# Modulation's accumulators transposed whole, its adds on VectorE alone, and the norms' tiles in strict order

## The chip, the cores and the metric

The kernel runs on one core of a Trainium2 chip. TensorE (PE) multiplies, VectorE (DVE), ScalarE (ACT) and GpSimd (POOL) work on tiles in SBUF, the first two also on PSUM, and SyncE (SP) issues most DMAs. Each engine takes its instructions strictly in the order in which the program lists them; a wait of one instruction holds up all behind it on that engine. The metric is the device time of one execution in microseconds (us).

## The reference

Two layers work on 512 latent tokens (`x`) and 256 context tokens (`ctx`), 1024 channels, all float32. Each layer is a half-step SwiGLU FFN, a token mixer (convolution, pooling, attention) and a second half-step FFN; before each comes a modulated RMS norm. The change touches how the modulation is computed and when the norms' tiles are made:

```python
m  = (jax.nn.silu(c)     @ w_mod[l] + b_mod[l]).reshape(B, N_MOD, D_MODEL)   # 1024 x 9216 weights a layer
mc = (jax.nn.silu(c_ctx) @ w_mod[l] + b_mod[l]).reshape(1, N_MOD, D_MODEL)
...
h = rms_norm(x, g) * (1 + m[:, 3*i + 1, None]) + m[:, 3*i, None]
x = x + 0.5 * m[:, 3*i + 2, None] * ((silu(a) * b) @ w2)        # a, b = split(h @ w1)
```

`m` and `mc` are matrix-vector products: two vectors (`c` and `c_ctx`) against the same 18 blocks of 512 columns in each layer.

## The kernel before

All activations lie transposed, as 8 tiles of 128 channels by 768 tokens. A product is made of three passes of a rounded type, so each operand is split into a high part (ScalarE casts) and a low part (VectorE subtracts): weights `stg` into `hl`, normed activations into `hhi` and `hlo`, the FFN's hidden values, which go through DRAM (`u`, `tmp` -> `gd` -> `gr`), into `gs`.

One FFN runs in stages. `ffn_in_first` and `ffn_in` make the first tiles of 128 hidden columns plainly, 96 matmuls of 512 or 256 columns a tile; `ffn_quad` makes the later ones with 7 products of half the tokens in place of 8, 84 matmuls of 384 columns a tile, from sums of token halves (`t0` to `t3`) that `sums_open` builds on VectorE (tag "T", tiles `tu` and `t`). `plain(l, s)` says where the quads begin: after tile 4 in the very first FFN, after tile 3 in the next two; the last FFN, which has no context tokens, is plain throughout. Then `ffn_out_main` multiplies 18 of the 22 hidden tiles by w2: two passes over 4 output tiles each, 18 x 2 x 4 = 144 groups of 6 matmuls (three of 512 columns, three of 256). In this text a main is one such stage of one of the first three FFNs. `ffn_out_last` adds the last 4 hidden tiles, updates `x` tile by tile and starts the next norms.

The modulation runs beside the first three FFNs, except 4 blocks that `start` makes at the beginning. `mod_chain` walks 12, 10 and 10 blocks in them. A block is 16 steps, 8 slices of 128 rows of w_mod times 2 vectors: each step multiplies a slice `wm` (128 x 512) by a column of silu(c) and adds it to an accumulator `acc` (128 x 2 x 512). The two steps of the first slice are written by ScalarE; the others are one SCALAR_TENSOR_TENSOR on VectorE, or, in the mains alone and where GpSimd has nothing to do, a product on ScalarE into `mt` and an add on GpSimd. `mod_fold` then sums `acc` over its 128 partitions: two DMAs on SP's queue bring one half of the partitions beside the other, two adds of 64 partitions on VectorE halve it (`fold`), 4 transposes on TensorE turn it into one PSUM bank (`mbank` in a main), and one TENSOR_REDUCE of 512 columns makes the 8 sums (`small`), which `mod_put` writes to `M`. All blocks of an FFN have to be done before its `ffn_out_last`: `flush_tag("mod")` stands at the end of `ffn_out_main`.

The order of instructions is made when the program is built. `Clock` estimates when each engine is free, and `Builder` keeps a heap of events (`at`, `after`, `defer`) that it takes as the estimated time goes by (`take`); an event for "DVE" is put off while VectorE is booked. Tags say what an event belongs to: "mod", "T", ("norm", stream). The streams of the norms are XA and XB (256 latent tokens each) and C (context), of falling priority in `PRIO`. On the chip no such choice is left: what the builder put in a row stays in it. All engines' calls pass through one helper, so every instruction has line 68, and rows are told apart by their tiles.

Of the kernel before, what the change touches and what calls it, by code (L numbers as in the profile page):

```python
# [16 lines left out]
P = 128  # L17
# [189 lines left out]
class Builder:  # L207
# [3 lines left out]
    def __init__(self, tc, nc, ins, out):  # L211
# [16 lines left out]
        self.spreads = 0  # L228

# [53 lines left out]
    def take(self, e):  # L283
        t, _, tag, fn, eng = e
        if eng is not None:
# [3 lines left out]
            if tag == "mod" and any(e[2] == "T" or e[2] in self.PRIO for e in self.events):  # L289

                self.at(max(t, self.now()) + 0.5, fn, tag, eng)
                return
# [48 lines left out]
    def plain(self, l, s):  # L341
        return NF - 1 if l == s == 1 else PLAIN + 1 + (l + s == 0)
# [227 lines left out]
    def mod_add(self, acc, k, v, src, pool=False):  # L570
# [4 lines left out]
        elif pool:  # L575
            t = self.tile(self.gopool, [P, 512], "mt", 2)
            nc.scalar.activation(t, src, AF.Copy, scale=sc)
            nc.gpsimd.tensor_tensor(acc[:, v], acc[:, v], t, OP.add)
        else:
            nc.vector.scalar_tensor_tensor(out=acc[:, v], in0=src, scalar=sc, in1=acc[:, v], op0=OP.mult, op1=OP.add)  # L580

    def mod_fold(self, l, cb, acc, then):

        nc = self.nc
        f = self.tile(self.wm_pool, [P, 512], "fold", 1)
        lower, upper = HALVES
        nc.sync.dma_start(f[lower], acc[upper, 0])
        nc.sync.dma_start(f[upper], acc[lower, 1])
        self.folds += 1

        def add():
            nc.vector.tensor_tensor(f[lower], f[lower], acc[lower, 0], OP.add)
            nc.vector.tensor_tensor(f[upper], f[upper], acc[upper, 1], OP.add)
            self.after([f], turn, "mod", 4.0)

        def turn():
            ps = self.mbank if self.mbank is not None else self.bank()
            self.hold(ps)
            self.transposes(ps, [f[:, b * P:(b + 1) * P] for b in range(4)])
            self.after([ps], lambda: put(ps), "mod")  # L600

        def put(ps):
            r = self.small(8).rearrange("p (v b) -> p v b", v=2)
            nc.vector.tensor_reduce(r, ps.rearrange("p (b v c) -> p v b c", b=4, v=2), axis=AX.X, op=OP.add)
            self.hold(ps, -1)
            self.mod_put(l, cb * 4, 4, r)
            self.folds -= 1
        self.after([f], add, "mod", 2.0)
# [10 lines left out]
    def mod_chain(self, blocks):  # L619
# [10 lines left out]
        def add(i, pool=False):  # L630
# [3 lines left out]
            self.mod_add(acc[0], k, v, w[i // 4][:, k % 2, :], pool)  # L634
# [5 lines left out]
            else:  # L640
                self.after([acc[0]], lambda: self.mod_fold(l, cb, acc[0], lambda: then(i + 1)), "mod", 1.0)

        def then(i):
            if i == len(steps):
                return
            if i // 4 not in w or (i % 16 == 15 and self.folds):

                self.defer(0.5, lambda: then(i), "mod")
                return
# [1247 lines left out]
```

## Time and profile before

| what | value |
|---|---|
| time, 3 runs | median 2686.82 us (2681.61 to 2687.28) |
| the profiled execution | time 2688.29 us, span 2686.5 us, mean granted TensorE clock 0.976 |
| busy share of the span | PE 95%, DVE 74%, ACT 42%, POOL 16% |
| chain that ended last | PE 70%, DVE 15%, DMA 10%, the rest 5% |
| mains (windows used below) | 375 to 578, 1281 to 1464, 1850 to 2018 us |

The profiled execution is 1.5 us above the median. A granted clock of 1 is 2.4 GHz; what TensorE gets otherwise is 1.2 GHz, so a mean of 0.92 over a stretch says that it had the lower level for 16% of it. The page counts a PE that is busy with pipelined matmuls as busy, whatever their pace.

### The profile page before, as it was taken

How to read it: one execution, taken by the hardware profiler on the slowest of the kernel's cores; microseconds unless marked ns; L12 is line 12 of the kernel's file. 1: busy time of each engine (PE TensorE's matmuls, PEld its weight loads, DVE VectorE, ACT ScalarE, POOL GpSimd, SP SyncE). 2: the span in 40 equal slices, each digit the busy share in tenths (PEclk: the TensorE clock that was granted, in tenths of full speed). 3: DMA queues.
4: the chain of work that ended last, by engine and by line, in shares of the span. 5: the costliest groups of instructions: out<-in, count | busy, mean ns of one | idle time of the engine just before them, and what ended most of it. 6: DMA issues, size and time to landing. Idle time of an engine off the chain costs nothing.

```text
span 2686.5 us, 40400 instructions
## 1 busy us (share of the span) xinstructions
PE 2543.1 (95%) x15100; PEld 2315.4 (86%) x15100; DVE 1982.2 (74%) x3553; ACT 1135.0 (42%) x2251; POOL 416.8 (16%) x460
## 2 busy tenths in 40 slices
PE   7999998879998999999989899999999999999998
PEld 4999987769987999999778899998788987888886
DVE  7888878767778698888777888887887787633355
ACT  4433335435445444333443443334454554422332
POOL 1000014341110200000332100002242111000001
PEclk9999999989999999999999899999999999999999
DMA  8334476734322343435765234347762422333362
GB/s 321 108 120 137 129 265 212 219 108 138 100 75 77 105 151 107 133 120 191 260 204 167 99 112 128 121 146 259 226 218 69 134 92 73 130 123 120 122 200 91
DMA packets 138133, 397.03 MB, mean 148 GB/s; under 512 B 15888, under 2 KB 34448, under 8 KB 136912
## 3 DMA queue, kind: packets, MB, share of 16 engines
q1 hardware_dynamic: 127728, 362.72, 42.0%
q0 software_dynamic: 10208, 31.73, 3.1%
q8 instruction: 118, 1.93, 0.3%
q14 instruction: 79, 0.65, 0.1%
HBM read 334.35 MB, written 53.22 MB: 144 GB/s over the span
## 4 chain that ended last, share of the span: by engine, by line
PE 70%; DVE 15%; DMA 10%; issue 2%; ACT 2%; SPq 1%; DVEq 0%; POOL 0%; ACTq 0%
PE b L68 70%; DMA gr<-gd 7%; DVE hl L68 3%; DVE acc L68 2%; DVE gs L68 2%; DMA wm<-in_wm_dram 1%; DVE hlo L68 1%; DVE small L68 1%; DVE x L68 1%; DVE tmph L68 1%; ACT gs L68 1%; DVE tu L68 1%; DVE fold L68 1%; SPq L68 1%; DMA x<-xd 1%
## 5 line engine op out<-in xcount | busy, mean ns | idle before, releaser
L68 PE MATMUL b<-hhi,hl 128*128 128x256 f32 (+2 forms) x4408 | 1145.7, 340 | 15.4 <-ACT hhi L68 7.0
L68 PEld LDWEIGHTS b<-hhi,hl 128*128 128x128 f32 x4408 | 776.4, 191 | 82.2 <-ACT hhi L68 8.2
L68 PE MATMUL b<-hlo,hl 128*128 128x512 f32 (+2 forms) x2204 | 731.0, 337 | 1.3 <-DVE hlo L68 1.2
L68 PE MATMUL b<-gs,hl 128*128 128x512 f32 (+1 forms) x3888 | 707.5, 343 | 10.9 <-DVE gs L68 4.4
L68 PEld LDWEIGHTS b<-gs,hl 128*128 128x128 f32 x3888 | 608.0, 193 | 101.8 <-DVE gs L68 6.6
L68 DVE TENSOR_TENSOR hl<-stg,hl 128x512 fp32r<-128x512 f32 x762 | 553.2, 746 | 117.1 <-ACT hl L68 116.2
L68 ACT CAST hl<-stg 128x512 fp32r<-128x512 f32 x762 | 450.5, 618 | 390.4 <-PE b L68 306.8
L68 PE MATMUL b<-t,hl 128*128 128x384 f32 x2544 | 468.0, 340 | 0.0
L68 PEld LDWEIGHTS b<-t,hl 128*128 128x128 f32 x2544 | 449.7, 188 | 0.2 <-DVE u L68 0.2
L68 PEld LDWEIGHTS b<-hlo,hl 128*128 128x128 f32 x2204 | 420.8, 191 | 31.8 <-DVE hlo L68 2.6
L68 DVE SCALAR_TENSOR_TENSOR acc<-wm,sc,acc 128x512 f32<-128x512 f32 x312 | 267.7, 873 | 30.0 <-DMA wm<-in_wm_dram 20.4
L68 ACT CAST gs<-gr 128x768 fp32r<-128x768 f32 (+1 forms) x160 | 124.7, 780 | 346.1 <-DMA gr<-gd 312.1
L68 DVE TENSOR_TENSOR gs<-gr,gs 128x768 fp32r<-128x768 f32 (+1 forms) x160 | 166.7, 1047 | 139.3 <-ACT gs L68 138.8
L68 POOL TENSOR_TENSOR acc<-acc,mt 128x512 f32<-128x512 f32 x136 | 206.7, 1522 | 293.9 <-ACT mt L68 251.8
L68 POOL DMA_DIRECT2D gd<-u x106 | 57.3, 541 | 729.4 <-DVE u L68 728.9
L68 DVE TENSOR_TENSOR u<-u,b 128x384 f32<-128x384 f32 x159 | 87.8, 552 | 86.0 <-PE b L68 85.0
L68 POOL TENSOR_TENSOR sqs<-sqs,tmph 128x256 f32<-128x256 f32 x102 | 79.2, 791 | 348.9 <-ACT tmph L68 347.4
L68 DVE SCALAR_TENSOR_TENSOR x<-b,M,x 128x256 f32<-128x256 f32 (+1 forms) x160 | 87.3, 571 | 56.6 <-PE b L68 56.1
L68 ACT ACTIVATE mt<-wm,sc 128x512 f32<-128x512 f32 x136 | 95.7, 718 | 52.9 <-DMA wm<-in_wm_dram 46.6
L68 POOL TENSOR_TENSOR bt<-E,con 128x256 f32<-128x256 f32 x64 | 47.2, 738 | 393.8 <-DVE small L68 339.5
L68 POOL DMA_DIRECT2D gd<-tmp x35 | 19.1, 547 | 445.1 <-DVE tmp L68 431.5
L68 DVE TENSOR_REDUCE small<-b 128x1 f32<-128x256 f32 (+5 forms) x130 | 63.4, 487 | 33.2 <-PE b L68 32.4
(117 smaller groups left out, 2050.5 us busy)
## 6 DMA issues: line engine op xcount, KB each, us to landing
stg<-in_w_dram SPq DMA_DIRECT2D x328, 512.0 KB
wm<-in_wm_dram SPq DMA_DIRECT2D x128, 512.0 KB
gr<-gd SPq DMA_DIRECT2D x120, 384.0 KB
gd<-u POOLq DMA_DIRECT2D x106, 192.0 KB, 2.2
xd<-x SPq DMA_DIRECT2D x32, 384.0 KB
x<-xd SPq DMA_DIRECT2D x32, 384.0 KB
gr<-gd SPq DMA_DIRECT2D x40, 256.0 KB
gd<-tmp POOLq DMA_DIRECT2D x35, 256.0 KB, 3.6
```

Source lines behind the costliest of these rows:

```text
L68: return f(*a, **k)
```

## The change

In three places it does this. The modulation's adds after the first slice are all on VectorE: the product on ScalarE into `mt` and the add on GpSimd are gone, and with them the rule in `mod_chain` that chose them. `mod_fold` makes no fold: `acc` is transposed as it is, 4 transposes and one TENSOR_REDUCE for the first vector, then 4 and one for the second, in a main both in the one bank `mbank`. The norms: while a stream's tiles are being made, events for VectorE of a lower priority (other streams' tiles, the token sums, modulation) are put off, at most three low parts (`rest`) are left pending, and the builds of the token sums are events for VectorE like the tiles. In the first FFN one tile more is plain, 5 where there were 4.

```diff
@@ -286,9 +288,10 @@
             if self.nc.end[eng] > max(t, self.now()) + (1.2 if tag in self.PRIO else 0.2):
                 self.at(self.nc.end[eng], fn, tag, eng)
                 return
-            if tag == "mod" and any(e[2] == "T" or e[2] in self.PRIO for e in self.events):
-
-                self.at(max(t, self.now()) + 0.5, fn, tag, eng)
+            if tag == "mod" and any(e[2] == "T" or e[2] in self.PRIO for e in self.events) \
+                    or any(self.PRIO.get(tag, 9) > self.PRIO[o] for o in self.tiling):
+
+                self.at(max(t, self.now()) + 0.4, fn, tag, eng)
                 return
         if eng is not None and tag in self.PRIO:
 
@@ -339,7 +342,7 @@
             self.take(heapq.heappop(self.events))
 
     def plain(self, l, s):
-        return NF - 1 if l == s == 1 else PLAIN + 1 + (l + s == 0)
+        return NF - 1 if l == s == 1 else PLAIN + 1 + 2 * (l + s == 0)
...
-    def mod_add(self, acc, k, v, src, pool=False):
+    def mod_add(self, acc, k, v, src):
         nc = self.nc
         sc = self.sc[:, 2 * k + v: 2 * k + v + 1]
         if k == 0:
             nc.scalar.activation(acc[:, v], src, AF.Copy, scale=sc)
-        elif pool:
-            t = self.tile(self.gopool, [P, 512], "mt", 2)
-            nc.scalar.activation(t, src, AF.Copy, scale=sc)
-            nc.gpsimd.tensor_tensor(acc[:, v], acc[:, v], t, OP.add)
         else:
             nc.vector.scalar_tensor_tensor(out=acc[:, v], in0=src, scalar=sc, in1=acc[:, v], op0=OP.mult, op1=OP.add)
 
     def mod_fold(self, l, cb, acc, then):
...
-        f = self.tile(self.wm_pool, [P, 512], "fold", 1)
-        lower, upper = HALVES
-        nc.sync.dma_start(f[lower], acc[upper, 0])
-        nc.sync.dma_start(f[upper], acc[lower, 1])
+        r = self.small(8).rearrange("p (v b) -> p v b", v=2)
         self.folds += 1
 
-        def add():
-            nc.vector.tensor_tensor(f[lower], f[lower], acc[lower, 0], OP.add)
-            nc.vector.tensor_tensor(f[upper], f[upper], acc[upper, 1], OP.add)
-            self.after([f], turn, "mod", 4.0)
-
-        def turn():
+        def turn(v):
             ps = self.mbank if self.mbank is not None else self.bank()
             self.hold(ps)
-            self.transposes(ps, [f[:, b * P:(b + 1) * P] for b in range(4)])
-            self.after([ps], lambda: put(ps), "mod")
-
-        def put(ps):
-            r = self.small(8).rearrange("p (v b) -> p v b", v=2)
-            nc.vector.tensor_reduce(r, ps.rearrange("p (b v c) -> p v b c", b=4, v=2), axis=AX.X, op=OP.add)
+            self.transposes(ps, [acc[:, v, b * P:(b + 1) * P] for b in range(4)])
+            self.after([ps], lambda: put(v, ps), "mod")
+
+        def put(v, ps):
+            nc.vector.tensor_reduce(r[:, v], ps.rearrange("p (b c) -> p b c", b=4), axis=AX.X, op=OP.add)
             self.hold(ps, -1)
-            self.mod_put(l, cb * 4, 4, r)
-            self.folds -= 1
-        self.after([f], add, "mod", 2.0)
+            if v == 0:
+                self.defer(0.0, lambda: turn(1), "mod")
+            else:
+                self.mod_put(l, cb * 4, 4, r)
+                self.folds -= 1
+        self.after([acc], lambda: turn(0), "mod", 3.0)
...
-            if self.mbank is not None and i % 16 > 1 and self.nc.end["POOL"] < self.now() + 0.2:
-
-                self.after([w[i // 4]], lambda: add(i, True), "mod", self.MSTEP)
-                return
             self.after([w[i // 4]], lambda: add(i), "mod", self.MSTEP, "DVE")
...
         def tiles(bc, k):
+            while len(self.rests) > 2:
+                self.rests[0]()
             rest, hi = self.norm_tile(l, i, st, bc, k)
-            self.after([hi], rest, tag)
+
+            def once():
+
+                if once in self.rests:
+                    self.rests.remove(once)
+                    rest()
+            self.rests.append(once)
+            self.after([hi], once, tag)
             if k + 1 < KT:
                 self.defer(0.0, lambda: tiles(bc, k + 1), tag, "DVE")
             else:
                 self.spreads -= 1
+                self.tiling.discard(tag)
...
+            self.tiling.add(tag)
...
         def build(kk):
             if not (ready(kk) and ready(kk + 4)) or (kk > 1 and (3, kk) not in self.t_sum):
-                self.defer(0.5, lambda: build(kk), "T")
+                self.defer(0.5, lambda: build(kk), "T", "DVE")
...
-                        build(kk + 1)
+                        self.defer(0.0, lambda: build(kk + 1), "T", "DVE")
...
-        self.defer(0.0, lambda: build(0), "T")
+        self.defer(0.0, lambda: build(0), "T", "DVE")
```

TensorE, in the second main, where a block's sums are turned. Before: `acc`'s fold goes into the bank b_5295 between two groups of the product (b_5296, b_5297 and b_5302 are outputs, gs a hidden tile, hl its weights).

```order
L68 MATMUL b_5296_12876<-gs_13068,hl_12886 128x512
L68 MATMUL b_5302_12882<-gs_13068,hl_12886 128x256
L68 MATMUL b_5295_12875<-con,fold_13122 128x128 x4
L68 MATMUL b_5297_12877<-gs_13068,hl_12886 128x512 x2
L68 MATMUL b_5302_12882<-gs_13068,hl_12886 128x256 x2
L68 MATMUL b_5297_12877<-gs_13068,hl_12886 128x512
L68 MATMUL b_5302_12882<-gs_13068,hl_12886 128x256
```

After: the block's `acc` goes into the bank b_5289 twice.

```order
L68 MATMUL b_5301_12787<-gs_12843,hl_12584 128x256
L68 MATMUL b_5289_12776<-con,acc_12750 128x128 x4
L68 MATMUL b_5291_12778<-gs_12843,hl_12584 128x512 x2
L68 MATMUL b_5301_12787<-gs_12843,hl_12584 128x256 x2
L68 MATMUL b_5291_12778<-gs_12843,hl_12584 128x512
L68 MATMUL b_5301_12787<-gs_12843,hl_12584 128x256
L68 MATMUL b_5289_12776<-con,acc_12750 128x128 x4
L68 MATMUL b_5294_12781<-gs_12843,hl_12584 128x512 x2
```

The second four transposes stand six matmuls behind the first and write the same bank.

VectorE, the same main. Before, from the fold of one block to its sums; acc_13132 is the next block's accumulator:

```order
L68 SCALAR_TENSOR_TENSOR acc_13132<-wm_13112,sc,acc_13132 128x512
L68 TENSOR_TENSOR hl_13153<-stg_12940,hl_13153 128x512
L68 TENSOR_TENSOR fold_13122<-fold_13122,acc_12858 64x512 x2
L68 TENSOR_TENSOR gs_13114<-gr_13115,gs_13114 128x768
L68 TENSOR_TENSOR gs_13154<-gr_13155,gs_13154 128x768
L68 SCALAR_TENSOR_TENSOR acc_13132<-wm_13112,sc,acc_13132 128x512
L68 TENSOR_TENSOR hl_13231<-stg_12940,hl_13231 128x512
L68 TENSOR_TENSOR hl_13232<-stg_12998,hl_13232 128x512
L68 TENSOR_TENSOR gs_13200<-gr_13201,gs_13200 128x768
L68 TENSOR_REDUCE small_13269<-b_5295_12875 128x8
L68 TENSOR_TENSOR M_78<-small_13269,par 128x2x4
L68 SCALAR_TENSOR_TENSOR M_78<-M_78,par 128x2x4
```

After, from the last add of a block (acc_12750) to its sums:

```order
L68 SCALAR_TENSOR_TENSOR acc_12750<-wm_12886,sc,acc_12750 128x512
L68 TENSOR_TENSOR hl_12953<-stg_12605,hl_12953 128x512
L68 TENSOR_TENSOR hl_12954<-stg_12822,hl_12954 128x512
L68 TENSOR_TENSOR gs_12918<-gr_12919,gs_12918 128x768
L68 SCALAR_TENSOR_TENSOR acc_12983<-wm_12933,sc,acc_12983 128x512
L68 TENSOR_TENSOR gs_12955<-gr_12956,gs_12955 128x768
L68 SCALAR_TENSOR_TENSOR acc_12983<-wm_12933,sc,acc_12983 128x512
L68 TENSOR_REDUCE small_12976<-b_5289_12776 128x4
L68 SCALAR_TENSOR_TENSOR acc_12983<-wm_12985,sc,acc_12983 128x512
L68 TENSOR_REDUCE small_12976<-b_5289_12776 128x4
L68 TENSOR_TENSOR M_78<-small_12976,par 128x2x4
L68 SCALAR_TENSOR_TENSOR M_78<-M_78,par 128x2x4
```

The adds of `fold` are gone, the reduce of 8 sums is two of 4 with an add of the next block (acc_12983) between them, and the next block has three adds in the stretch where it had two. Counted in the whole order from the first to the last `gs` of a main, VectorE makes 53, 41 and 42 adds to `acc` before and 97, 84 and 84 after, and 9, 7 and 7 reduces before and 16, 14 and 14 after. Ahead of the mains, beside the first stages of the FFN, it makes 60, 56 and 60 adds before and 71, 56 and 56 after.

VectorE at the end of the first main. After the change, the last rows ahead of `ffn_out_last`: the x rows update the stream from the finished banks, and the two reduces of the last block stand behind six of its adds.

```order
L68 SCALAR_TENSOR_TENSOR x_3533<-b_1872_4430,M_77,x_3533 128x512
L68 SCALAR_TENSOR_TENSOR x_3532<-b_1873_4431,M_77,x_3532 128x256
L68 SCALAR_TENSOR_TENSOR x_3533<-b_1873_4431,M_77,x_3533 128x256
L68 SCALAR_TENSOR_TENSOR acc_5001<-wm_5054,sc,acc_5001 128x512 x2
L68 SCALAR_TENSOR_TENSOR acc_5001<-wm_5102,sc,acc_5001 128x512 x4
L68 TENSOR_REDUCE small_5158<-b_1868_4426 128x4 x2
L68 TENSOR_TENSOR M_77<-small_5158,par 128x2x4
```

Before, four adds of `acc`, the two adds of `fold` and one reduce stood in their place.

VectorE in the norms ahead of the third FFN (bc_14777 is stream XB in the rows of before, bc_14752 stream C in those of after; tu and t are the token sums). Before:

```order
L68 TENSOR_TENSOR tu_15180<-tu_15180,tu_15182 128x384
L68 TENSOR_TENSOR tu_15182<-tu_15182,tu_15181 128x384
L68 TENSOR_TENSOR tu_15181<-tu_15181,tu_15180 128x384
L68 TENSOR_TENSOR tu_15183<-tu_15183,tu_15181 128x384
L68 SCALAR_TENSOR_TENSOR tmph_15198<-x_12734,M_78,bc_14777 128x256
L68 SCALAR_TENSOR_TENSOR tmph_15201<-x_12735,M_78,bc_14777 128x256
L68 SCALAR_TENSOR_TENSOR hlo_93<-tmph_15198,M_78,hhi_85 128x256
L68 SCALAR_TENSOR_TENSOR hlo_94<-tmph_15201,M_78,hhi_86 128x256
L68 SCALAR_TENSOR_TENSOR tmph_15211<-x_12734,M_78,bc_14951 128x256
L68 SCALAR_TENSOR_TENSOR tmph_15214<-x_12735,M_78,bc_14951 128x256
```

After:

```order
L68 SCALAR_TENSOR_TENSOR tmph_14965<-x_12624,M_78,bc_14752 128x256
L68 SCALAR_TENSOR_TENSOR tmph_14968<-x_12625,M_78,bc_14752 128x256
L68 SCALAR_TENSOR_TENSOR hlo_92<-tmph_14945,M_78,hhi_84 128x256
L68 SCALAR_TENSOR_TENSOR hlo_93<-tmph_14965,M_78,hhi_85 128x256
L68 SCALAR_TENSOR_TENSOR hlo_94<-tmph_14968,M_78,hhi_86 128x256
L68 TENSOR_TENSOR tu_15007<-hhi_79,hlo_87 128x384
L68 TENSOR_TENSOR tu_15005<-hhi_79,hlo_87 128x384
L68 TENSOR_TENSOR tu_15006<-hhi_83,hlo_91 128x384
```

Before, the last two tiles of XB (x_12734, x_12735) stood behind the first build of token sums and the eight `tu` of the second, 20 instructions; after, all tiles of all three streams stand ahead of the first build.

## Rows read from the trace of the kernel before

**Rows 1.** Who PE waited for, whole kernel: total us, times, longest.
```profile
PE b L68 <- DVE fold L68: 60.4, 16, 12.4
```

**Rows 2.** Timeline 576 to 581 us: start, us, engine, instruction [idle before, releaser].
```profile
578.06 1.12 PE L68 MATMUL b<-con,fold 128*128 128x128 f32 x4 [12.39 <-DVE fold L68]
```

**Rows 3.** Four windows: busy us (instructions) by engine, PEclk, DMA share, GB/s.
```profile
375.00:578.00 203.00, 163.66 (x896) 141.21 (x894) 165.55 (x181) 93.62 (x144) 85.72 (x57) 0.92 0.69 221
1281.00:1464.00 183.00, 162.76 (x894) 140.88 (x893) 144.17 (x161) 86.34 (x133) 64.33 (x45) 0.95 0.67 217
1850.00:2018.00 168.00, 156.62 (x886) 134.94 (x886) 137.69 (x157) 79.73 (x121) 59.96 (x40) 0.99 0.72 231
200.00:300.00 100.00, 100.00 (x574) 99.96 (x573) 84.00 (x144) 37.87 (x69) 6.50 (x12) 1.00 0.40 127
```

**Rows 4.** VectorE by form, 250 to 350 us: count | busy, mean ns | idle before.
```profile
L68 DVE TENSOR_TENSOR hl<-stg,hl 128x512 fp32r<-128x512 f32 x41 | 28.1, 684 | 0.0
L68 DVE SCALAR_TENSOR_TENSOR acc<-wm,sc,acc 128x512 f32<-128x512 f32 x24 | 17.4, 745 | 0.0
L68 DVE TENSOR_REDUCE small<-b 128x8 f32<-128x512 f32 x2 | 1.4, 692 | 1.1 <-PE b L68 1.1
```

**Rows 5.** Timeline 1300 to 1302 us.
```profile
1300.12 0.74 DVE L68 SCALAR_TENSOR_TENSOR acc<-wm,sc,acc 128x512 f32<-128x512 f32 x1
1300.78 0.95 DVE L68 TENSOR_TENSOR gs<-gr,gs 128x768 fp32r<-128x768 f32 x1
1301.32 1.55 POOL L68 TENSOR_TENSOR acc<-acc,mt 128x512 f32<-128x512 f32 x1 [3.35 <-ACT mt L68]
1301.65 1.78 DVE L68 SCALAR_TENSOR_TENSOR acc<-wm,sc,acc 128x512 f32<-128x512 f32 x1
```

**Rows 6.** VectorE by form, 375 to 578 us.
```profile
L68 DVE SCALAR_TENSOR_TENSOR acc<-wm,sc,acc 128x512 f32<-128x512 f32 x51 | 51.1, 1008 | 9.8 <-DMA wm<-in_wm_dram 7.7 <-POOL acc L68 1.3 <-ACT acc L68 0.6
L68 DVE TENSOR_TENSOR gs<-gr,gs 128x768 fp32r<-128x768 f32 x37 | 48.6, 1317 | 14.6 <-ACT gs L68 14.5
L68 DVE TENSOR_TENSOR hl<-stg,hl 128x512 fp32r<-128x512 f32 x38 | 38.1, 1040 | 0.5 <-ACT hl L68 0.5
L68 DVE TENSOR_TENSOR fold<-fold,acc 64x512 f32<-64x512 f32 x18 | 15.3, 851 | 12.6 <-DMA fold<-acc 12.3
```

**Rows 7.** VectorE by form, 1281 to 1464 us.
```profile
L68 DVE SCALAR_TENSOR_TENSOR acc<-wm,sc,acc 128x512 f32<-128x512 f32 x41 | 43.7, 1071 | 6.1 <-ACT acc L68 4.8 <-POOL acc L68 1.2
L68 DVE TENSOR_TENSOR gs<-gr,gs 128x768 fp32r<-128x768 f32 x37 | 41.6, 1130 | 30.0 <-ACT gs L68 29.9
L68 DVE TENSOR_TENSOR hl<-stg,hl 128x512 fp32r<-128x512 f32 x38 | 35.3, 967 | 0.9 <-ACT hl L68 0.8
L68 DVE TENSOR_TENSOR fold<-fold,acc 64x512 f32<-64x512 f32 x14 | 13.8, 982 | 6.0 <-DMA fold<-acc 5.7
```

**Rows 8.** VectorE by form, 1850 to 2018 us.
```profile
L68 DVE SCALAR_TENSOR_TENSOR acc<-wm,sc,acc 128x512 f32<-128x512 f32 x40 | 42.5, 1076 | 6.3 <-DMA wm<-in_wm_dram 4.9 <-POOL acc L68 1.2 <-ACT acc L68 0.3
L68 DVE TENSOR_TENSOR gs<-gr,gs 128x768 fp32r<-128x768 f32 x37 | 40.6, 1102 | 19.2 <-ACT gs L68 19.0
L68 DVE TENSOR_TENSOR hl<-stg,hl 128x512 fp32r<-128x512 f32 x38 | 35.7, 974 | 2.3 <-ACT hl L68 2.3
L68 DVE TENSOR_TENSOR fold<-fold,acc 64x512 f32<-64x512 f32 x12 | 10.2, 852 | 2.6 <-DMA fold<-acc 2.2
```

**Rows 9.** ScalarE by form, 375 to 578 us.
```profile
L68 ACT ACTIVATE mt<-wm,sc 128x512 f32<-128x512 f32 x55 | 38.6, 718 | 31.5 <-DMA wm<-in_wm_dram 27.3 <-POOL acc L68 4.0
```

**Rows 10.** Timeline of PE, 175.5 to 176.5 us.
```profile
175.63 0.60 PE L68 MATMUL b<-con,fold 128*128 128x128 f32 x4
175.99 0.77 PE L68 MATMUL b<-t,hl 128*128 128x384 f32 x3
```

**Rows 11.** Timeline 1527 to 1536 us.
```profile
1529.92 2.33 DVE L68 TENSOR_TENSOR tu<-tu,tu 128x384 f32<-128x384 f32 x4
1533.23 0.58 PE L68 MATMUL b<-hhi,hl 128*128 128x256 f32 x1 [4.88 <-ACT hhi L68]
```

More of the change, by code (lines that the diff above doesn't have):

```diff
@@ L228, in __init__ @@
         self.spreads = 0
+        self.tiling = set()
+        self.rests = []
         self.folds = 0
@@ L628, in load, with add @@
                 w[q] = self.mod_load(*blocks[q // 4], q % 4)
-        def add(i, pool=False):
+        def add(i):
             l, cb, k, v = steps[i]
@@ L633, in add @@
                 acc[0] = self.mod_acc(4)
-            self.mod_add(acc[0], k, v, w[i // 4][:, k % 2, :], pool)
+            self.mod_add(acc[0], k, v, w[i // 4][:, k % 2, :])
             if i % 4 == 3:
@@ L640, in add @@
             else:
-                self.after([acc[0]], lambda: self.mod_fold(l, cb, acc[0], lambda: then(i + 1)), "mod", 1.0)
+                self.after([acc[0]], lambda: self.mod_fold(l, cb, acc[0], lambda: then(i + 1)), "mod")
         def then(i):
```

## The prediction

> **What bounds the kernel now.** The span of 2686.5 us lies 1.8 us under its execution's time of 2688.29, which is 1.5 above the median of the runs shown; the sum is made against 2688.3 and moved by 1.5 at the end. I looked first at who makes TensorE wait. One name stands out: 16 waits for `fold`, 60.4 us, the longest 12.4 [rows 1], which ended at 578 us [rows 2]. Then I asked where they lie, by windows. In the quads (200 to 300) PE is busy in every microsecond at full clock and makes 574 matmuls, 0.174 us each for 384 columns [rows 3]. A main is 144 groups of 2304 columns, six times 384, so 144 x 6 x 0.174 = 150.5 us of TensorE. The three mains last 203, 183 and 168, 554 in all [rows 3]: 102 us are lost there, in waits and at the lower clock (granted 0.92, 0.95 and 0.99, that is 16%, 10% and 2% of the time at 1.2 GHz). Nothing like this is lost beside the quads, where the same folds stand.
>
> What TensorE waits for is late because VectorE is. VectorE is busy for 165.6, 144.2 and 137.7 us of the mains [rows 3], and nearly all its idle time there is waiting for loads, for ScalarE behind a load, or for the fold's DMA [rows 6 to 8]; TensorE holds these forms up nowhere. So VectorE sets the pace of the mains, and the reader is to see why. Beside the quads an add to `acc` takes 745 ns and a low part `hl` 684 [rows 4]. In the mains the same forms take 1008 to 1076 and 967 to 1040 [rows 6 to 8]. The timeline shows how: an add that starts at 1300.12 takes 0.74; the next starts at 1301.65, when GpSimd has been in an add of 1.55 us since 1301.32, and takes 1.78 [rows 5]. Each of GpSimd's adds costs VectorE about as much as it saves.
>
> **VectorE in the mains.** I take from each main's busy time what its forms cost above their undisturbed price, 745 and 684 ns [rows 4] and 0.95 us for `gs` [rows 5]. Main one [rows 6]: 51 x 0.263 + 37 x 0.367 + 38 x 0.356 = 40.5 us. Main two [rows 7]: 41 x 0.326 + 37 x 0.180 + 38 x 0.283 = 30.9. Main three [rows 8]: 40 x 0.331 + 37 x 0.152 + 38 x 0.290 = 29.8. That is 101 us, and it goes with GpSimd's adds if these cause it. The fold's adds go as they are: 15.3, 13.8 and 10.2 [rows 6 to 8]. What comes: 44, 43 and 42 more adds of VectorE by the order, each 0.66 from its start to the next start [rows 5], 29.0, 28.4 and 27.7; and 7 more reduces a main, of 256 in place of 512 columns in effect, at most the 0.69 of today's [rows 4], 4.8. Busy time after: 143.6, 132.7 and 130.2.
>
> Idle before were 37.4, 38.8 and 30.3 (window less busy, [rows 3]). The waits for the fold's DMA in it, 12.6, 6.0 and 2.6 [rows 6 to 8], cannot recur; 24.8, 32.8 and 27.7 remain, as `gr` and `wm` loads come as late as before. With them VectorE needs 168, 166 and 158 us.
>
> **TensorE in the mains.** 150.5 us, and two sets of four transposes a block at 0.36 [rows 10], 16, 14 and 14 sets by the order: 5.8, 5.0 and 5.0. At the end of the first main the last block is not done, and PE cannot go on before its second set: behind the last group stand three x updates and six adds on VectorE, nine at some 0.66, then 0.60 for transposes, 0.69, and 0.36 again: 7.5 us, where 12.4 stand today [rows 2]. In the other two the last block is done ahead of the x updates. The one bank: a second set may start when the first has passed (0.60, [rows 10]) and been reduced (0.69), 1.3 us; six matmuls and the first set's issue cover 1.04 + 0.36. It fits if VectorE comes to the reduce at once; behind one `gs` it is 0.95 late. So 0 to 0.95 us for each of 22 blocks; I take 0.35, for VectorE is busy but its rows there are short, 2.6 us a main. TensorE needs 166, 158 and 158.
>
> I take 172, 165 and 160: a little above the larger of the two in the first, where both are full and the load of `wm` may now be felt on VectorE (ScalarE waited 31.5 us ahead of its 55 products, [rows 9], at no one's cost), between them in the second, where VectorE has slack again, above both in the third. Against 203, 183 and 168 this is **-31, -18 and -8, together -57 us**.
>
> By the Trainium skill's page "SBUF — State Buffer", section "Who interferes with whom", a VectorE instruction with two inputs in SBUF contends with a GpSimd instruction that reads SBUF, and nothing else in SBUF does; by that all of the 101 us would go, as I have it. By its page "Perfetto Trace Analysis", section "Identifying the Most-Contended Engine", occupancy is a fair measure for VectorE of how near it is to its limit; taken at its word, the busy time of [rows 3] is all work and the new adds come on top, which is the slower case below. The pair of adds in [rows 5] speaks for the first.
>
> **The rest.** One plain tile of 96 matmuls for a quad of 84: 12 x 0.174 = +2.1 us, all on the path, since PE is full there [rows 3]; VectorE, with 16 us idle in 100 there, covers what it gets. The 10 blocks outside the mains get four transposes more: 10 x 0.36 = +3.6, for the same reason; two banks are used there, so no wait is added. The 11 adds more ahead of the first main are 7 us of VectorE in some 250, inside its idle time. If that cover were gone they would cost these 7. Norms: ahead of the third FFN, TensorE waits 4.88 us for the tile whose input VectorE made only after the token sums [rows 11]; the new order puts the tile first. I take -4, with 0 (another tile is late instead) and -7 (some lower clock behind it goes too) as bounds. What is late next there are the token sums, by some 3 us; TensorE has three streams of two tiles and a plain tile to do ahead of the first use, 3 x 96 x 0.116 + 16.7 = 50 us by the pace above. ScalarE loses its 136 products and SP its 64 fold DMAs; neither is a bound, so nothing is counted.
>
> Sum: -57 + 2.1 + 3.6 - 4 = -55; 2688.3 - 55 = 2633, and 1.5 less for the median: **2632 us**.
>
> **The rivals.**
> *Loads take over.* VectorE runs nearer to its loads, and the first add of each `wm` and each `gs` stands and waits in its queue. For it: waits of 24.8 to 32.8 us a main are there already, and [rows 9] shows 31.5 more on ScalarE. Against: DMA share is 0.67 to 0.72 in the mains [rows 3], and fewer bytes move. With waits half as long again, VectorE needs 181, 182 and 172: -22, -1, +4; with the rest -17, **2670**.
> *The shared bank.* Each reduce is found behind something, and every block costs TensorE the whole 1.3 us of transposes and reduce: 22 x 1.3 - 7.7 = 21 more than forecast, **2653**. Against: the order has six matmuls between the sets. The Trainium skill's page "Perfetto Trace Analysis", section "Matmuls", says that independent groups should rotate through PSUM banks so that one's evacuation overlaps the next; by that this place is built wrongly, and the time is this rival's.
> *Slower: VectorE is stretched by something else.* If GpSimd's adds are not what stretches VectorE's forms, the 101 us stay and the mains need 168.4 + 40.5, 165.5 + 30.9 and 157.9 + 29.8: 209, 196 and 188, +39 together; with the rest +41, **2728**. It decides from 62% of the 101 us on (by VectorE's account the mains fall from 554 to 492, 62 us). Against it: the same forms keep their price beside the quads, where GpSimd adds nothing.
>
> **How the numbers follow.** The forecast gets 0.66, loads 0.17, the bank 0.10, slower 0.07. 2632 is the likeliest case's; its own range runs from both limits met (164, 156 and 156 in the mains, norms -7: 2607) to 2650. With loads and bank the range is 2605 to 2668; below lies little, above the slower case and the tail of the loads. About 0.2%, 5.4 us, is what a measurement of this kernel tells from no change. Forecast, bank and all but the tail of the loads are faster: 0.89; that tail gives 0.04 for the same; slower 0.07.
>
> **What would show it.** Right: in windows from the first to the last group, mains of about 172, 165 and 160 us with granted clock near 1; `hl` at 684 and adds at 745 ns in them; no `fold`, and waits of PE for `acc` and `small` of under 20 us in all, the longest at the end of the first main; the 4.88 us before the third FFN gone. Wrong: `hl` still at 1000 ns in the mains (slower), VectorE's waits ahead of `gs` and `acc` over 100 us there (loads), or a wait of 1 us ahead of each second set (bank).

## The result and the profile after

The changed kernel takes 2639.86 us (median of 4 runs, 2637.89 to 2647.21), beside it the kernel before 2684.22: a ratio of 0.984 with a 95% interval of 0.9816 to 0.9864. The forecast was 2632 with a range of 2605 to 2668. It is faster, as forecast, and the time is 8 us above the one forecast. The profiled execution is the slowest of the four, 2647.21 us with a span of 2645.4, 41 us below the profiled one of before; its busy shares are PE 96%, DVE 73%, ACT 40% and POOL 8%, its mean granted clock 0.984.

The same windows as [rows 3], the three mains and a stretch of quads (busy us and instructions of PE, PEld, DVE, ACT, POOL; granted clock; DMA share; GB/s). As before, a main ends 36 us before the last product of w2:

```profile
380.50:556.00 175.50, 161.09 (x921) 139.55 (x920) 139.99 (x210) 59.74 (x90) 1.09 (x2) 0.98 0.68 228
1261.00:1425.00 164.00, 157.18 (x906) 137.30 (x906) 129.68 (x195) 57.55 (x88) 1.08 (x2) 0.99 0.69 230
1809.00:1976.00 167.00, 159.44 (x914) 138.52 (x913) 129.07 (x195) 58.39 (x89) 1.08 (x2) 0.99 0.67 227
200.00:300.00 100.00, 100.00 (x579) 99.86 (x578) 83.68 (x144) 39.59 (x72) 7.50 (x14) 1.00 0.39 128
```

The mains fell from 203, 183 and 168 us to 175.5, 164 and 167. VectorE is busy for 140, 130 and 129 us of them where the account forecast 143.6, 132.7 and 130.2, and idle for 35.5, 34.3 and 37.9 (window less busy) where it carried over 24.8, 32.8 and 27.7. By form, first and third main (count | busy, mean ns | idle before), against [rows 6] and [rows 8]:

```profile
L68 DVE SCALAR_TENSOR_TENSOR acc<-wm,sc,acc 128x512 f32<-128x512 f32 x96 | 67.5, 744 | 7.5 <-DMA wm<-in_wm_dram 7.5
L68 DVE TENSOR_TENSOR gs<-gr,gs 128x768 fp32r<-128x768 f32 x37 | 35.2, 955 | 25.7 <-ACT gs L68 25.5
L68 DVE TENSOR_TENSOR hl<-stg,hl 128x512 fp32r<-128x512 f32 x38 | 24.4, 683 | 0.2 <-ACT hl L68 0.2
...
L68 DVE SCALAR_TENSOR_TENSOR acc<-wm,sc,acc 128x512 f32<-128x512 f32 x83 | 58.6, 745 | 2.1 <-DMA wm<-in_wm_dram 2.1
L68 DVE TENSOR_TENSOR gs<-gr,gs 128x768 fp32r<-128x768 f32 x37 | 35.2, 955 | 33.4 <-ACT gs L68 33.4
L68 DVE TENSOR_TENSOR hl<-stg,hl 128x512 fp32r<-128x512 f32 x38 | 24.4, 683 | 0.0
```

The stretch is gone: an add costs 744 ns where it cost 1008 to 1076, a low part 683 where it cost 967 to 1040. That settles the slower rival. Who TensorE waits for, whole kernel (total, times, longest), against [rows 1]:

```profile
PE b L68 <- DVE small L68: 24.3, 15, 4.3
PE b L68 <- DVE acc L68: 4.8, 1, 4.8
```

The 60.4 us for `fold` are gone, and 17.7 of these 24.3 lie in the mains, ahead of second sets of transposes: 12 of the 19 there wait, 0.6 to 4.3 us. The longest, on the timeline of VectorE and PE (start, us, instruction, idle before and its releaser):

```profile
1282.81 0.60 PE L68 MATMUL b<-con,acc 128*128 128x128 f32 x4
...
1284.23 0.95 DVE L68 TENSOR_TENSOR gs<-gr,gs 128x768 fp32r<-128x768 f32 x1
1285.10 0.75 DVE L68 SCALAR_TENSOR_TENSOR acc<-wm,sc,acc 128x512 f32<-128x512 f32 x1
...
1286.50 0.96 DVE L68 TENSOR_TENSOR gs<-gr,gs 128x768 fp32r<-128x768 f32 x1 [0.66 <-ACT gs L68]
...
1288.04 0.68 DVE L68 TENSOR_REDUCE small<-b 128x4 f32<-128x512 f32 x1
...
1288.78 1.12 PE L68 MATMUL b<-con,acc 128*128 128x128 f32 x4 [4.31 <-DVE small L68]
```

The 10 us behind it, as windows of 5:

```profile
1289.00:1294.00 5.00, 5.00 (x23) 4.39 (x23) 4.15 (x8) 2.37 (x4) 0.00 (x0) 0.69 0.62 209
1294.00:1299.00 5.00, 5.00 (x30) 4.40 (x30) 4.57 (x7) 1.51 (x3) 0.00 (x0) 1.00 0.74 257
```

The first set has passed at 1283.4, but its reduce stands behind low parts, adds and a `gs` that itself waits for a load, and comes at 1288. The wait is not all: in the next 5 us the granted clock is 0.69, and 23 matmuls are made where 30 are in the 5 after.

### The profile page after: what moved, and what is told of

Same layout as the page of the kernel before. It is cut to its first block, busy times and chain, and to the rows that moved or that the text cites. A ratio compares the mean times of both kernels' runs of the same rounds, so it can differ in the third digit from the quotient of the medians.

```text
span 2645.4 us, 40165 instructions
## 1 busy us (share of the span) xinstructions
PE 2545.9 (96%) x15240; PEld 2318.8 (88%) x15240; DVE 1926.1 (73%) x3645; ACT 1047.6 (40%) x2111; POOL 210.8 (8%) x324
## 4 chain that ended last, share of the span: by engine, by line
PE 75%; DMA 10%; DVE 10%; ACT 2%; issue 2%; SPq 1%; ACTq 0%; POOL 0%; DVEq 0%; POOLq 0%
PE b L68 75%; DMA gr<-gd 9%; DVE hl L68 3%; DVE gs L68 2%; DVE acc L68 1%; ACT gs L68 1%; DMA wm<-in_wm_dram 1%; DVE small L68 1%; DVE hlo L68 1%; SPq L68 1%; DVE p L68 1%; DVE x L68 0%; DVE tmph L68 0%; DVE tmp L68 0%; ACT hl L68 0%
## 5 line engine op out<-in xcount | busy, mean ns | idle before, releaser
L68 PE MATMUL b<-hhi,hl 128*128 128x512 f32 (+2 forms) x4448 | 1157.7, 340 | 9.2 <-DVE hl L68 3.9
L68 PE MATMUL b<-hlo,hl 128*128 128x256 f32 (+2 forms) x2224 | 737.6, 337 | 0.9 <-DVE hlo L68 0.9
L68 PE MATMUL b<-gs,hl 128*128 128x512 f32 (+1 forms) x3888 | 697.9, 340 | 7.1 <-DVE tmp L68 2.7
L68 DVE TENSOR_TENSOR hl<-stg,hl 128x512 fp32r<-128x512 f32 x760 | 514.3, 698 | 115.1 <-ACT hl L68 113.9
L68 DVE SCALAR_TENSOR_TENSOR acc<-wm,sc,acc 128x512 f32<-128x512 f32 x448 | 318.5, 745 | 17.9 <-DMA wm<-in_wm_dram 11.6
L68 DVE TENSOR_TENSOR gs<-gr,gs 128x768 fp32r<-128x768 f32 (+1 forms) x160 | 141.5, 889 | 162.8 <-ACT gs L68 162.2
L68 DVE TENSOR_REDUCE small<-b 128x4 f32<-128x512 f32 (+4 forms) x162 | 85.4, 527 | 38.0 <-PE b L68 36.7
L68 PE MATMUL b<-hl,hhi 128*128 128x256 f32 x384 | 74.8, 294 | 3.8 <-ACT hhi L68 3.8
L68 ACT ACTIVATE p<-p,small 128x256 f32<-128x256 f32 x64 | 32.7, 511 | 111.1 <-DVE small L68 108.4
L68 DVE TENSOR_TENSOR stg<-stg 128x512 f32<-128x512 f32 x104 | 72.0, 692 | 3.6
## 6 DMA issues: line engine op xcount, KB each, us to landing
gd<-u POOLq DMA_DIRECT2D x104, 192.0 KB, 2.2
```

Of the source, the lines that this page charges most:

```text
L68: return f(*a, **k)
```

## The experiments

Ratios are to the kernel before in the same set of runs; stages and idle time are of one profiled execution each. "Stages" are from the first to the last product of w2 in the first three FFNs (a main and some 36 us), as the timeline has them; PE idle is TensorE's idle time up to its last instruction.

| kernel | median us (lowest to highest) | ratio to before, 95% | stages us | PE idle |
|---|---|---|---|---|
| before | 2684 to 2688 in five sets | 1 | 240.5, 219.4, 204.5 | 137 |
| changed | 2639.9 (2637.9 to 2647.2) | 0.9816 to 0.9864 | 211.8, 200.5, 203.2 | 93 |
| e1 no GpSimd adds | 2676.2 (2671.3 to 2677.8) | 0.9946 to 0.9971 | 236.6, 206.1, 202.8 | 134 |
| e2 no fold | 2680.4 (2674.5 to 2688.4) | 0.9968 to 0.9996 | 229.7, 213.0, 213.4 | 127 |
| e3 norms | 2682.6 (2680.4 to 2685.7) | 0.9973 to 0.9993 | 241.4, 203.6, 216.2 | 133 |
| e4 plain tile | 2679.2 (2674.5 to 2683.0) | 0.9959 to 0.9980 | 225.6, 217.3, 209.4 | 125 |
| e10 e1 and e2 together | 2657.9 (2656.3 to 2659.8) | 0.9882 to 0.9915 | 223.1, 205.4, 200.5 | 105 |
| e11 changed, 4 plain tiles | 2643.1 (2639.8 to 2647.6) | 0.9823 to 0.9865 | 214.7, 197.2, 202.1 | 92 |
| e5 second set later | 2641.9 (2638.7 to 2643.2) | 0.9814 to 0.9845 | 210.1, 199.0, 199.8 | 91 |
| e6 ones | 2641.4 (2639.9 to 2643.6) | 0.9814 to 0.9845 | 201.6, 196.9, 196.9 | 68 |
| e9 three load buffers | 2641.6 (2639.2 to 2642.7) | 0.9814 to 0.9845 | 207.2, 201.5, 203.6 | 90 |
| e7 idle GpSimd adds | 2773.9 (2772.8 to 2775.0) | 1.0307 to 1.0338 | 254.7, 246.1, 242.3 | 195 |
| e12 two banks | 2630.1 (2628.8 to 2634.8) | 0.9778 to 0.9817 | 209.1, 192.1, 198.4 | 82 |
| e13 two banks, 6 plain tiles | 2612.5 (2611.7 to 2617.1) | 0.9709 to 0.9749 | 192.0, 191.6, 194.6 | 66 |

### The parts alone (e1 to e4)

**e1**, the kernel before without the rule that gives adds to GpSimd:

```diff
-            if self.mbank is not None and i % 16 > 1 and self.nc.end["POOL"] < self.now() + 0.2:
-
-                self.after([w[i // 4]], lambda: add(i, True), "mod", self.MSTEP)
-                return
```

> The kernel before with one part of the change: GpSimd makes no adds, the fold stays as it was. Theory A (GpSimd's adds stretch VectorE, and VectorE paces the mains): low parts at 684 and adds at 745 ns in the mains; by the prediction's account VectorE loses 40.5, 30.9 and 29.8 us there and gets 29, 28 and 28, so with its old idle time the mains are 191, 181 and 166 us, about 16 us less in all (ratio 0.994). Theory B (the fold is late only because VectorE is stretched): with the stretch gone the waits for fold shrink from 60 us to under 20, and this part alone gives 35 to 45 us (ratio about 0.985). Rival: GpSimd's share of the adds was worth what it cost, 0 or slower.

It took 11 us less, near theory A's 16; B falls. The low parts are at 685 ns in the first main with the fold still there, so it is GpSimd's adds that stretched them. Main by main theory A's account does not hold: it gives 12, 2 and 2 us less, and the stages are 4, 13 and 2 shorter. The 57.6 us for `fold` are as many as before, but in 6 waits, and three of them follow each other at the end of the first main:

```profile
550.49 1.12 PE L68 MATMUL b<-con,fold 128*128 128x128 f32 x4 [15.71 <-DVE fold L68]
...
556.93 1.33 ACT L68 ACTIVATE acc<-wm,sc 128x512 f32<-128x512 f32 x2 [19.90 <-DMA wm<-in_wm_dram]
...
566.01 1.11 PE L68 MATMUL b<-con,fold 128*128 128x128 f32 x4 [14.41 <-DVE fold L68]
...
575.56 1.11 PE L68 MATMUL b<-con,fold 128*128 128x128 f32 x4 [8.43 <-DVE fold L68]
```

TensorE has no product left there that may go ahead of them. What it waits for is a chain with one thing at a time in it: load, adds, the fold's DMA, its adds, the turn, the next block. VectorE is no longer stretched, but in the first main the blocks still end after the products.

**e2**, `mod_fold` as in the change, GpSimd's adds kept.

> The kernel before with one part of the change: the accumulators are transposed whole, GpSimd keeps its adds. Theory A: VectorE loses 39 us of fold adds and 21 us of waiting for the fold's DMA in the mains and gets some 14 us of reduces: about 46 us less (ratio 0.983), low parts still near 1000 ns. Theory B: with VectorE still stretched, each second set of transposes finds its reduce late, and the gain is 10 to 25 us (ratio 0.991 to 0.996).

5 us less by the ratio, 7 by the medians: theory A's 46 fall, and theory B's 10 to 25 as well. What B says of the waits is so: TensorE's waits for the reduce take the place of those for `fold` (total, times, longest):

```profile
PE b L68 <- DVE small L68: 52.8, 20, 6.5
PE b L68 <- DVE acc L68: 9.2, 1, 9.2
```

**e3**, the change's order of norms and token sums alone.

> The kernel before with the order of norms and token sums alone. By the prediction 4 us less, from the wait of 4.88 us ahead of the third FFN (0 to 7 less). Rival, read from the trace after the change: that stretch is 7 us shorter and the quads behind it are 4 us longer because the token sums come later, so 2 us less or none (ratio 0.999 to 1.000).

4.6 us less. From the second to the third stage 345.8 us pass where 349.9 did: the forecast -4, in its place. But the second stage is 16 us shorter and the third 12 longer, though no rule for the work in them differs except by when an event is tried again. The third has nine adds more in it, on VectorE and GpSimd together (87 where 78 were); the second has 84 as before.

**e4**, the fifth plain tile alone (`2 * (l + s == 0)` in `plain`).

> The kernel before with the fifth plain tile in the first FFN alone. By the prediction 2.1 us more (ratio 1.001), 12 matmuls at 0.174. Rival: the first product of w2 begins 5.8 us later in the trace after the change, of which the transposes are 1.4 and the plain tile would be up to 4.4 (ratio 1.002).

Both fall: it is 8 us faster. The first w2 product starts 2.9 us later, where 2.1 was forecast, and the first stage is 15 us shorter: a quad tile costs VectorE seven rows of `u` at 0.55 us, two of `stg` at 0.69 and two low parts at 0.68 that a plain tile does not, some 6.6 us in all, and VectorE has that much more of the modulation done when the stage starts (50 and 48 adds in it, where 51 and 55 were, on VectorE and GpSimd).

**e10**, e1 and e2 in one kernel.

> The kernel before with two parts of the change together: no adds on GpSimd and no fold; the norms and the plain tiles as before. Alone the first gave 11 us and the second 5. If the parts are independent: 16 us less than before (ratio 0.994). If they need each other (without GpSimd the chain of blocks ends late and the fold's way by DMA stands at the end of each main; with the stretch the second set finds its reduce late): 30 to 38 us less (ratio 0.986 to 0.989).

28 us less (2657.9 beside 2685.9), 10 to 12 more than the two alone add up to and just short of the second expectation: the two parts need each other. Who TensorE waits for, whole kernel:

```profile
PE b L68 <- DVE small L68: 28.7, 16, 5.3
PE b L68 <- DVE acc L68: 13.2, 2, 9.0
```

**e11** is the changed kernel with `(l + s == 0)` in place of `2 * (l + s == 0)`, so e10, the norms' order and one line more, which the section on the change leaves out and e2 and e10 do not have: the builder lets no 1 us of its estimated time pass any more between a block's last add and what follows it (its sums and the next block).

```diff
-                self.after([acc[0]], lambda: self.mod_fold(l, cb, acc[0], lambda: then(i + 1)), "mod", 1.0)
+                self.after([acc[0]], lambda: self.mod_fold(l, cb, acc[0], lambda: then(i + 1)), "mod")
```

> The changed kernel with four plain tiles in the first FFN, as before. By the prediction's +2.1 us for the fifth it is 2 us faster than the changed kernel (2638). Rival, from the plain tile alone on the kernel before (8 us less, the first main with a block less to do): the adds that lay beside the plain tile go back into the first main, its end comes later, and it is 4 to 10 us slower (2644 to 2650).

2643.1 beside 2639.9, with runs that overlap: not told apart. From e10 to e11 the norms' order and that 1 us together are worth 15 us by the medians. In the traces 3.6 us lie between the second and third stage and 8.4 and 8.2 in the first two, whose waits of TensorE fall from 24.6 to 16.6 and from 9.8 to 3.9; the third is 1.6 longer. No run has one of the two without the other on e10, so which of them the 15 us belong to is not shown. On the kernel before, the norms' order alone (e3) left the first stage as it was, with the same 106 adds in it; from e10 to e11 they go from 102 to 98.

### What the stretch costs (e7)

```diff
+            if self.mbank is not None and i % 16 > 1 and self.nc.end["POOL"] < self.now() + 0.2:
...
+                t = self.idle["t"]
+                self.nc.gpsimd.tensor_tensor(t, t, t, OP.add)
             self.after([w[i // 4]], lambda: add(i), "mod", self.MSTEP, "DVE")
```

> The changed kernel with GpSimd adds put back that nobody waits for: wherever the kernel before would have given GpSimd an add, it adds a tile of its own to itself, 128 x 512. Theory A (the stretch of VectorE sets the mains): low parts back near 1000 ns, VectorE's busy time up by 70 to 100 us and the mains longer by as much as the account says, 60 to 90 us (2700 to 2730). Rival, from the run with the fold and no GpSimd (101 us of stretch gone, 11 us gained): most of the stretch lies in VectorE's idle time or at places where TensorE does not wait: 10 to 40 us (2650 to 2680).

134 us more than the changed kernel: theory A's way, and above its size, since GpSimd made 250 such adds where it had 136 before (nobody takes the turn from VectorE, so more steps find it idle). GpSimd's adds in the whole kernel, and VectorE by form in the first main and its end, 380 to 599 us:

```profile
L68 POOL TENSOR_TENSOR mt<-mt 128x512 f32<-128x512 f32 x250 | 355.3, 1421 | 19.6
...
L68 DVE SCALAR_TENSOR_TENSOR acc<-wm,sc,acc 128x512 f32<-128x512 f32 x96 | 101.5, 1098 | 3.3 <-DMA wm<-in_wm_dram 3.3
L68 DVE TENSOR_TENSOR gs<-gr,gs 128x768 fp32r<-128x768 f32 x37 | 51.2, 1388 | 9.3 <-ACT gs L68 9.2
L68 DVE TENSOR_TENSOR hl<-stg,hl 128x512 fp32r<-128x512 f32 x38 | 40.1, 1095 | 0.0
L68 DVE TENSOR_REDUCE small<-b 128x4 f32<-128x512 f32 x14 | 9.6, 683 | 1.9 <-PE b L68 1.8
L68 DVE SCALAR_TENSOR_TENSOR x<-b,M,x 128x512 f32<-128x512 f32 x8 | 5.9, 742 | 2.2 <-PE b L68 2.2
```

Here 96 x 0.354 + 37 x 0.433 + 38 x 0.412 = 66 us of stretch stand in one main, and the stage is 43 longer. So the stretch is GpSimd's, and here, with VectorE busy for 205 of the 219 us, it costs time. Reduces and the x updates, which read PSUM, keep their price. By the Trainium skill's page "SBUF — State Buffer", section "Who interferes with whom", a VectorE instruction with at most one input in SBUF does not contend with GpSimd, outside the modes in which it uses two ports; the rows agree (683 and 742 ns).

### What keeps the mains above the forecast (e5, e6, e9, e12, e13)

**e5**: `self.defer(3.0, lambda: turn(1), "mod")` in place of 0.0.

> The changed kernel with each block's second four transposes issued 3 us later on TensorE. In its trace they wait 17.7 us in the mains for the reduce of the first, and a set behind a wait takes 1.12 us where one without takes 0.60 and has the next matmul 0.36 behind it. If the shared bank is what keeps the mains 9 us above the forecast: most of these waits go, 12 to 20 us less (2620 to 2628). Rival: VectorE is late there in any case and the wait comes back at the next block or at the end of the main: within 4 us of the changed kernel.

**e9**: three `gr` buffers, and loads issued one tile earlier.

> The changed kernel with three buffers for the hidden tiles' loads (gr) in place of two, each load issued one tile earlier. If the loads take over (VectorE waits 25.7, 28.5 and 33.4 us for gs behind a gr load in the mains): these waits halve, and TensorE's waits for small with them: 5 to 15 us less than the changed kernel. Rival (VectorE's waits there lie in slack): within 4 us.

**e6**: in `mod_fold`

```diff
-            self.transposes(ps, [acc[:, v, b * P:(b + 1) * P] for b in range(4)])
...
-            nc.vector.tensor_reduce(r[:, v], ps.rearrange("p (b c) -> p b c", b=4), axis=AX.X, op=OP.add)
+            for v in range(2):
+                for b in range(4):
+                    j = 4 * v + b
+                    nc.tensor.matmul(ps[:, j:j + 1], acc[:, v, b * P:(b + 1) * P], self.ones, start=j == 0, stop=j == 7, skip_group_check=True)
```

> The changed kernel with no transposes and no reduce: the accumulator's eight tiles are each multiplied by a column of ones, eight matmuls of one column into eight columns of one bank, and the sums are read from there. VectorE loses 2 x 0.69 us a block, some 8 us a main, and nothing waits for a reduce. If the bank and VectorE's load hold the mains: 15 to 28 us less than the changed kernel (2612 to 2625), waits of TensorE for small gone. Rival: eight matmuls of one column cost as much as eight transposes and the mains stay at TensorE's own need: 5 to 10 less.

All three are at 2641 to 2642 us, not told apart from the changed kernel. For e5 and e9 that is what their rivals say; e6 gives neither of its two. They are not the same inside. e9 does not halve what it was to halve: VectorE's waits for `gs` go from 25.7, 28.7 and 33.4 us to 26.6, 23.1 and 26.1, and TensorE's for `small` from 17.7 to 21.8. So it says little of the loads rival; e13 below decides that. In e5 the waits for `small` go from 17.7 to 9.1 us, but the wait at the end of the first main grows from 4.8 to 11.8. In e6 TensorE waits 2.4 us in all three stages; but a block costs it 1.70 us, from 1301.15 to 1302.85, where eight transposes cost 0.71:

```profile
1301.15 1.84 PE L68 MATMUL b<-ones,acc 128*128 128x1 f32 x16
1302.85 1.54 PE L68 MATMUL b<-gs,hl 128*128 128x512 f32 x7
```

Eight products of one column run as 16 matmuls, and 32 blocks x 0.99 us = 32 us is paid for 27 us of waits in the stages and the clock behind them.

**e12**: two banks in a main, one for each vector, all eight transposes together.

```diff
-            ps = self.mbank if self.mbank is not None else self.bank()
+            ps = self.mbank[v] if self.mbank is not None else self.bank()
...
+            if v == 0 and self.mbank is not None:
+                turn(1)
...
+                self.mbank = [m0, self.bank()]
```

> The changed kernel with two banks for a block's sums in the mains, so that the eight transposes stand together and no set waits for a reduce. In the run with ones the stages with w2 took 201.6, 196.9 and 196.9 us with TensorE never waiting, and each block cost TensorE 1.70 us there against 0.71 for eight transposes. Without waits the stages would be some 195, 191 and 191 where the changed kernel's profile has 211.8, 200.5 and 203.2: up to 39 us less; I expect 20 to 35 less than the changed kernel (2605 to 2620). Rival: VectorE is late in any case, the waits come back as waits for acc or for x at the ends: within 8 us of the changed kernel.

2630.1: 10 us less, between the two. No set waits for a reduce any more. The second stage is at 192.1 with 0.4 us of waits. The first still has 14, nearly all in one place, and larger than in the changed kernel:

```profile
544.18 4.05 DVE L68 SCALAR_TENSOR_TENSOR acc<-wm,sc,acc 128x512 f32<-128x512 f32 x6
549.30 2.74 DVE L68 SCALAR_TENSOR_TENSOR acc<-wm,sc,acc 128x512 f32<-128x512 f32 x4 [1.07 <-DMA wm<-in_wm_dram]
551.44 1.97 PE L68 MATMUL b<-con,acc 128*128 128x128 f32 x8 [13.43 <-DVE acc L68]
```

With TensorE sooner done, ten adds of the last block are left behind the last x update. **e13** is e12 with `3 * (l + s == 0)` in `plain`, a sixth plain tile.

> The kernel with two banks, and a sixth plain tile in the first FFN. With two banks TensorE waits 13.43 us at the end of the first main, for ten adds of the last block that stand behind the last x update; with a sixth plain tile the order has none there (84 adds ahead of the first product of w2 and 84 in it, where it had 71 and 97). If that tail is what is left: the wait goes, the tile costs 2.1, together 11 to 14 us less than with two banks (2616 to 2619). Rival: what VectorE does ahead of the main was not idle time, and the quads or the first product of w2 start later: within 4 us of two banks (2626 to 2634).

2612.5, 17.6 us less than e12 and 27 less than the changed kernel. In the traces the first stage starts 3.4 us later and is 17.1 shorter, for a wait of 13.4 and a granted clock that was 0.97 in it and is 1.00; the third is 3.8 shorter, and why is not shown. This version beats both kernels. What the sixth tile gives with one bank was not run. Its mains, and VectorE's `gs` in each:

```profile
383.00:539.00 156.00, 156.00 (x914) 137.35 (x913) 127.19 (x191) 57.88 (x88) 1.09 (x2) 1.00 0.72 233
1242.00:1397.00 155.00, 155.00 (x908) 136.49 (x907) 128.65 (x194) 57.71 (x87) 1.08 (x2) 1.00 0.72 240
1781.00:1939.50 158.50, 156.29 (x910) 136.72 (x909) 126.70 (x192) 57.67 (x88) 1.08 (x2) 1.00 0.70 233
...
L68 DVE TENSOR_TENSOR gs<-gr,gs 128x768 fp32r<-128x768 f32 x37 | 35.3, 955 | 27.2 <-ACT gs L68 27.2
L68 DVE TENSOR_TENSOR gs<-gr,gs 128x768 fp32r<-128x768 f32 x37 | 35.3, 956 | 24.3 <-ACT gs L68 24.2
L68 DVE TENSOR_TENSOR gs<-gr,gs 128x768 fp32r<-128x768 f32 x37 | 35.2, 955 | 31.4 <-ACT gs L68 31.2
```

TensorE is busy nearly throughout, at full clock: 155 to 158.5 us is what a main needs, and VectorE, busy for 127 to 129 and idle for the rest, is no limit. It still waits 24 to 31 us for `gs`, that is for loads, and TensorE does not feel it: the loads rival falls here.

## Why the prediction was right, and where it was not

The time fell into the range, and into the likeliest case's own range (2607 to 2650). By medians the change is worth 44 to 48 us where 55 were forecast.

**Stretch and fold.** Right in what goes: 101 us of stretch, the fold's adds and its waits. Wrong as a price for each. By the account (busy time less the stretch, plus the idle time kept) GpSimd's part alone was worth 16 and measured 11, the fold's was worth 46 and measured 5. The two together bring what neither brings alone, 28 us (e10), but the forecast gave them 53, the mains' 57 less 3.6 for the transposes. Another 15 came with the norms' order, priced at 4, and the 1 us that the prediction does not name (e11). That the sum came out is in part luck.

**Mains: forecast -31, -18, -8.** Measured, by where the first and last w2 products lie, -29, -19 and -1. The first two are right in size, but not by the account: in e10 they are -17 and -14, and the rest came with the norms' order and the 1 us. VectorE's need in it is its busy time and the idle time of before, 168, 166 and 158 us; e13's second main takes 155 with the same work on VectorE (82 adds to `acc`, 83 in the changed kernel), so the idle time is no need. The end of the first main, forecast at 7.5 us (its terms add up to 7.6), is 4.82 of wait, a set, 0.79 of wait and a set: 7.5 from the last product at 548.76 to the next at 556.25. The third main failed. TensorE needed 156 (e13) and had, in 167, waits of 7.6 us, 4.3 of them for `small` and 2.5 for the gate's `tmp` at its start, and the clock behind them.

**The shared bank: the term that was mis-sized.** Taken at 0.35 us for each of 22 blocks, 7.7 in all; measured 17.7 us for the 19 blocks whose sets lie in the mains, 0.93 each, with the lower clock behind the long ones on top. The reduce is not found behind one `gs` at most, as the step had it, but behind whatever VectorE has in its row, a load included. In size it lies midway between the forecast's 7.7 and the 28.6 of the bank's rival (0.10), and with 12 of 19 second sets waiting the rival's sign, a wait of 1 us ahead of each, was half there. By the Trainium skill's page "Perfetto Trace Analysis", section "Matmuls", independent groups should rotate through PSUM banks; e12 agrees, with 10 us, and 27 with e13's tile to clear the end.

**Rest: forecast +1.7, measured +8** (the spans are 41 us apart, the stages 49). A set costs 0.355 us as forecast. The norms' -4 came where it was forecast (e3: -4.1; the 4.88 us gap is gone), and the third FFN's quads are 2.7 us longer than in e10, which has the old order (266.4 and 263.7). The token sums come late, but TensorE waits for them only 0.34 us, at 1525.65; 8 us later it waits 1.75 for a `u`, a row with which VectorE reads a quad's bank. The plain tile's +2.1 is right as a price and wrong as the tile's worth: ahead of the first main it frees VectorE for adds that would otherwise stand at its end, where nothing covers them (e4: 8 us faster; the cover that I named was not what counted). The profiled execution is 7.4 us above its kernel's median and the one of before 1.5 above its own, so up to 6 us of what is above the forecast may be this execution's own; in e9's trace the stretches between the stages are 3.0 us shorter in all.

**What would show it.** `hl` at 684, adds at 745, no `fold`, clock near 1, longest wait at the end of the first main: all seen. Waits for `acc` and `small` in the mains under 20 us: not met, 22.5. The sign of loads, over 100 us of VectorE's waits ahead of `gs` and `acc` there, was near, 97.5, and still not one of loads as a limit (e13).

**Open.** Why the norms' order and the 1 us move the first two mains by 8 us each (e10 to e11), and the norms' order the second by -16 and the third by +12 in e3, was not tried. What changes in them is where a block's steps fall among loads and long rows, which is argued and not shown. By e3 an edit that gives a main no rule of its own can take 16 us from one and add 12 to another, so a part's price in a single main is no firmer than that.

## What to carry to other kernels

A helper engine's adds are only worth their price if they don't stretch the engine they relieve; compare the same form with and without the neighbour before summing busy times. Where a serial chain has to end before the next stage, look at what is left of it when the main engine has run out of work: that tail is paid in full (13.4 us of wait in e12), and work moved ahead of the stage, even at a cost on the main engine, can buy it back. A bank that two groups share is priced by the row that stands ahead of its reader, not by the reader's own time.

## What the runs showed of the hardware

A GpSimd add of a private tile, 128 x 512, with which no instruction shares data, brings VectorE's adds from 744 to 1098 ns on average and its low parts from 683 to 1095, and leaves a form that reads PSUM at its price (e7). A product with one column of ones costs 1.70 us for eight tiles of 128 x 128, eight transposes and their 1024 columns 0.71. After a wait of 4.31 us TensorE's granted clock was 0.69 for the next 5 us, which is 1.2 GHz for 62% of them.
